# First block: gate2's second half on ScalarE and GpSimd, and the second routing pieces of both token tiles side by side

## The chip, the core and the metric

The kernel runs on one core of a Trainium2 chip. The metric is the device time of one execution in microseconds (us); the median of three runs is quoted, and one further execution was profiled. Engines are named as in the profile: PE (TensorE matmul), DVE (VectorE), ACT (ScalarE), POOL (GpSimd) and SP, whose queue issues nearly all loads from HBM.

## The reference, cut to what matters

Two blocks run one after the other over 256 tokens of width 1024. The first is attention and a pooling mixer, gated, followed by a mixture of 32 experts; the second is another mixer and an MLP, twice. The change touches the end of the first block's mixer, where the residual is formed, the router reads it, and the gate of the expert output is computed from the condition vector `c`.

```
mod = silu(c) @ w_ada + b_ada                       # six rows of 1024
shift1, scale1, gate1, shift2, scale2, gate2 = split(mod, 6)
...
x  = x + gate1 * (mixed @ w_out)
h2 = rms_norm(x, norm2_g) * (1 + scale2) + shift2
z_group, z_expert = h2 @ w_router_group + b, h2 @ w_router_expert + b
...                                                 # best group, best two of its eight experts
x  = x + gate2 * sum over the chosen experts e of weight_e * ((silu(h2 @ w_g[e]) * (h2 @ w_u[e])) @ w_d[e])
```

`gate2` is the vector c_act (1024) times a 1024 x 1024 slice of `w_ada`, computed in two halves of 512 columns. The routing needs, for each token, the sum of squares of the new x and 36 dot products of x with the router's weights.

## The kernel before, in words

Tokens stand on partitions in two tiles of 128 (t = 0, 1), and x has two column pieces of 512 (n = 0, 1). A float32 weight is split into a high part (`wh`, a cast on ACT, L206) and a low part (`wl`, a subtraction on DVE, L207), and each product is three matmuls: high with high (L230), low activation with high (L231), high activation with low weight (L232).

**Loads.** All weights pass through a ring of slots in SBUF, loaded by SP's queue in program order (`load_into`, L176). A slot is loaded again when its last reader is done, and SP waits in order: a load whose slot is still read holds every load behind it. While the first block's mixer (`phase_a`) still computes, the expert weights of `phase_b` are already being loaded, first the gate, up, gate and down matrices of the first experts (1 MB each), then 2 MB loads. The second 2 MB load of "up" goes into the slot that has held x until then (`self.xring`, added after `choose`), so it waits for the last reader of x.

**The end of phase_a.** The output projection `w_out` runs over two column pieces (c0 = 0, 512) and two halves of k. After each piece `evac_o` makes x: a product with gate1 (L723, reads PSUM) and a sum (L724). Between the matmuls the callback `both` advances two things: an order of steps (`start_route`, which makes the router's bias row zb from s2b, L867 and L870, then `route_piece` for n = 0 of both token tiles) and the generator `gate_sums` for gate2. For each half n of gate2 that generator lets GpSimd write the bias on a diagonal (L854, tile `gate2s`), then `ada_sum` loads two 1 MB parts of w_ada (four k rows each) and DVE adds eight scaled rows (L843, 128x512, one instruction per k row), and a matmul with ones (L858, `gb`) sums over partitions.

For c0 = 512 the last half of k is done token tile by token tile: t = 0 and its `evac_o`, t = 1 and its `evac_o`. Then `route_piece(t, 1, p)` runs for t = 0 and then t = 1: the sum of squares on ACT (`junk`, L270), four transposes on PE (`xt`, L884), a copy out of PSUM (`xa`, L886: on DVE for t = 0, on ACT for t = 1), four products with the router's weights (`lg`, L889), the reciprocal root on GpSimd (L278, L281), and the logits `z` on DVE (L892).

**The start of phase_b.** Four matmuls put x into the accumulators (`acc`, L986). `choose` picks experts on DVE (L906 to L927, result A); `slots` ranks tokens (L934 to L943). Then four ACT instructions make the high part of the normed x (L996), and four DVE instructions the low part (`low`, L1001): one behind A, three behind the comparison `sel` (L1041). After these the gather matmuls (`gx`, L1015) and the expert products run.

**Order of work.** Program order is only a priority: a scheduler places each instruction on its engine's queue where its own estimate of times has the engine free and the inputs ready. So on an engine a later step can stand before an earlier one. In the profile L854 for n = 1 stands on GpSimd directly behind that for n = 0, although eight DVE sums lie between them in program order, and L858 for n = 0 stands between the zb matmuls. `issue_after(ins)` puts an instruction behind `ins` on its engine. Once queued, each engine works strictly in order.

Of the kernel before, what the change touches and what calls it, by code (L numbers as in the profile page):

```python
# [11 lines left out]
F32 = mybir.dt.float32  # L12
# [4 lines left out]
AF = mybir.ActivationFunctionType  # L17
ALU = mybir.AluOpType
# [3 lines left out]
S = 256  # L22
D = 1024
# [92 lines left out]
class Kernel:  # L116
# [149 lines left out]
    def sumsq(self, x, ss, junk=None, scale=1.0):  # L266

        if junk is None:
            junk = self.sp.tile([128, D], F32R, name="junk", tag="wl")
        self.nc.scalar.activation(junk[:, 0:x.shape[1]], x, AF.Square, scale=scale, accum_out=ss)  # L270

    def rsqrt(self, ss, parts, n=D):

# [13 lines left out]
    def bank(self, shape=(128, 512), name="b"):  # L287
        return self.psum.tile(list(shape), F32, name=name, tag="b")
# [93 lines left out]
    def phase_a(self, rs):  # L382
        tc, nc, a = self.tc, self.nc, self.a
        with ExitStack() as st:
# [8 lines left out]
            p = s2.enter_context(tc.tile_pool(name="pa2", bufs=1, reuse_waits="tile"))  # L393
# [3 lines left out]
            bank = self.bank  # L397
# [11 lines left out]
            for t in range(2):  # L409
                ss = self.new_ss(1)  # L410
# [307 lines left out]
            p = st.enter_context(tc.tile_pool(name="pa3", bufs=1, reuse_waits="tile"))  # L718

            def evac_o(t, c0, ps):  # L720
                tmp = p.tile([128, 512], F32, name="otmp", tag="s", bufs=3)
                xx = self.x[:, t, c0:c0 + 512]
                nc.vector.tensor_tensor(tmp, ps, gate1[:, c0:c0 + 512], op=ALU.mult)  # L723
                nc.vector.tensor_tensor(xx, tmp, xx, op=ALU.add)  # L724


            self.gb = []
            sums = self.gate_sums(p.tile([128, D], F32, name="gate2s"), 10, lambda y, pb: self.gb.append(pb))

            def both():  # L730
                step()
# [3 lines left out]
            for c0 in (0, 512):  # L735
                ps = [bank() for _ in range(2)]
# [12 lines left out]
            for t in range(2):  # L749
                for k, hi, lo, off in parts:  # L750
                    self.tok_step1(ps[t], mT, 4 + k, t, hi[:, off:off + 512], lo[:, off:off + 512], False, k == 3)
                evac_o(t, 512, ps[t])
            for t in range(2):
                self.route_piece(t, 1, p)
    def load_rotary(self, p, tmp):
        a = self.a
        self.ind = self.cp.tile([128, 2], F32, name="ind")
        self.load_small(self.ind, a["k_rot"][:, 32:34])
        pos = p.tile([128, 2], I32, name="pos")
        self.load_small(pos, a["positions_2"].rearrange("o (t p) -> p (o t)", p=128))  # L760
        self.load_small(tmp[:, 194:226], a["k_rot"][:, 0:32])
        return pos, tmp
# [68 lines left out]
        self.row_cols(mod, pt, nb)  # L831
        self.nc.vector.tensor_reduce(dst, pt.rearrange("p b (i s r) -> p i b s r", s=2, r=32)[:, :, :, :, 0], axis=AX.X, op=ALU.add)

    def ada_sum(self, chunk, y, first):

        for i in range(2):
            v = self.ada_load(i, chunk)
            for kk in range(4):
                ck = self.cs[:, 4 * i + kk:4 * i + kk + 1]
                if first and i + kk == 0:  # L840
                    self.nc.vector.tensor_scalar(y, v[:, kk], ck, None, op0=ALU.mult)
                else:
                    self.nc.vector.scalar_tensor_tensor(y, v[:, kk], ck, y, op0=ALU.mult, op1=ALU.add)  # L843
                if kk % 2:
                    yield

    def gate_sums(self, gate, chunk, put):

        nc = self.nc
        c = self.vcol["b_ada", 16] + 4 * chunk - 16  # L850
        for n in range(2):
            y = gate[:, n * 512:(n + 1) * 512]

            nc.gpsimd.tensor_tensor(y.rearrange("p (b f) -> p b f", f=128), self.ident.unsqueeze(1).to_broadcast([128, 4, 128]),  # L854
                                    self.cols[:, c + 4 * n:c + 4 * n + 4].unsqueeze(2).to_broadcast([128, 4, 128]), op=ALU.mult)
            yield from self.ada_sum(chunk + n, y, False)
            pb = self.bank(name="gb")
            nc.tensor.matmul(pb, self.ones, y, start=True, stop=True)  # L858
            put(y, pb)
# [17 lines left out]
    def route_piece(self, t, n, p):  # L877

        nc, bank = self.nc, self.bank
        x = self.x[:, t, n * 512:n * 512 + 512]  # L880
        self.sumsq(x, self.ss1[t][:, n:n + 1])
        ps = bank((128, 4, 128), "xt")
        for b in range(4):
            nc.tensor.transpose(ps[:, b], self.strided(x, 4)[:, b], self.ident)  # L884
        xa = p.tile([128, 4, 128], F32, name="xa", tag="s", bufs=3)
        (nc.scalar.copy if t else nc.vector.tensor_copy)(xa, ps)  # L886
        for b in range(4):
            k = 4 * n + b
            nc.tensor.matmul(self.lg[t], xa[:, b], self.wr[:, k], start=k == 0, stop=k == 7)  # L889
        if n == 1:  # L890
            self.r1[t] = self.rsqrt(self.ss1[t], 2)
            nc.vector.scalar_tensor_tensor(self.z[:, t], self.lg[t], self.r1[t], self.br, op0=ALU.mult, op1=ALU.add)  # L892

    def choose(self, p):

# [77 lines left out]
    def phase_b(self, rs):  # L973
        tc, nc, a, misc = self.tc, self.nc, self.a, self.misc
        with ExitStack() as st:
            self.add_ring(rs, 1, side="right")
            p = st.enter_context(tc.tile_pool(name="pb", bufs=1, reuse_waits="tile"))
# [9 lines left out]
                                     skip_group_check=True)  # L987
            self.choose(p)
            Rm, cnt = self.slots(p)
            lows = []  # L990
            for n in range(2):
                for t in range(2):
                    xx = self.strided(self.x[:, t], 8)[:, 4 * n:4 * n + 4]
                    hi, lo = (self.hT.t[i][n][:, t] for i in range(2))
                    hi, lo = (v.rearrange("p (b c) -> p b c", b=4) if len(v.shape) == 2 else v for v in (hi, lo))
                    nc.scalar.activation(hi, xx, AF.Copy, scale=self.r1[t])  # L996
                    lows.append((lo, xx, self.r1[t], hi.bitcast(F32)))

            def low(after):
                with tc.issue_after(after):  # L1000
                    nc.vector.scalar_tensor_tensor(*lows.pop(0), op0=ALU.mult, op1=ALU.subtract)  # L1001

            low(self.after_A)

            self.add_slots(st, [self.xring])

# [29 lines left out]
            def choose_slots(pr):  # L1036

                b = pr // 2
                sel = [pw.tile([128, 4, 64], F32R, name="sel", tag=f"sel{t}") for t in range(2)]
                for t in range(2):  # L1040
                    cmp = nc.vector.tensor_tensor(sel[t], Rm[:, t, 4 * b:4 * b + 4].unsqueeze(2).to_broadcast([128, 4, 64]),  # L1041
                                                  misc[:, 0:64].unsqueeze(1).to_broadcast([128, 4, 64]), op=ALU.is_equal).ins
                while lows:
                    low(cmp)
                quad["sf"] = [s.rearrange("p e c -> p (e c)") for s in sel]
                quad["xT"] = pw.tile([128, 8, 256], F32, name="xT", tag="xT")

# [18 lines left out]
            def gate(pr):  # L1066

                pg = None
                if pr % 2 == 0:
                    choose_slots(pr)  # L1070
                for k in range(0, 10, 2):
                    if pr % 2 == 0 and k < 8:
                        gather(k)
                    if k:
                        if pg is None:
                            pg = self.bank((128, 512), "pg")
                        for kk in (k - 2, k - 1):
                            product(pg, weights["g", pr], pr, kk)
                    yield pg
# [822 lines left out]
```

## Time and profile before

| | us |
|---|---|
| Median of three runs | 1307.24 |
| Lowest and highest run | 1305.76, 1309.66 |
| The profiled execution | 1306.97 |
| Its span, first to last instruction | 1305.2 |
| Busy in the span: PE, DVE, ACT, POOL | 1253.0, 680.5, 510.7, 200.7 |
| HBM read in the span | 357.00 MB, 274 GB/s on average |

The times on the views count from the span's start. A timeline line gives the start, the duration, the engine, the line of code, the operation and "output<-inputs" with shapes; "x8" merges eight of a kind, and brackets at the end give idle time before it and what ended it. A windows line gives for a stretch the busy time of each engine with the number of instructions, then PE's granted clock as a share of full speed, the share of the DMA engines that were busy, and GB/s. A few records are missing from a trace of this kind, so counts on timelines can be one short.

### The profile page before, as it was taken

Reading aid. Unit: us, or ns where it says so; the run is one execution under the profiler, and the core shown is the slowest. Engines: PE = TensorE matmul, PEld = TensorE weight load, DVE = VectorE, ACT = ScalarE, POOL = GpSimd, SP = SyncE. Lnnn points to the kernel's source line nnn. Section 1 sums busy time; section 2 is a strip of 40 time slices with the busy share of each in tenths; the row PEclk is TensorE's granted clock in tenths of the full one; section 3 lists DMA queues with packets and bytes.
Section 4 is the critical chain, followed back from the end, with each engine's and each line's share of the span. In section 5 each row is a group of like instructions: output and inputs, shape, how many; then the busy total and the mean of one; then the engine's idle time right before and its main releaser. Section 6 shows DMA issues by size and latency. Waiting matters only on the chain. (4 is left out here: it accounts for less than half of the span.)

```text
span 1305.2 us, 19758 instructions
## 1 busy us (share of the span) xinstructions
PE 1253.0 (96%) x7985; PEld 875.2 (67%) x7985; DVE 680.5 (52%) x1164; ACT 510.7 (39%) x919; POOL 200.7 (15%) x270
## 2 busy tenths in 40 slices
PE   6999988999999999899999999999999999999997
PEld 3889976344443443333357678998988767989896
DVE  3698797122122221212157965655557994765654
ACT  2456433111110111101056465555556555655544
POOL 0011030000000000000024541211113461211211
PEclk9999998999999999999999999999999999999999
DMA  9998797999999999999975342655554423555550
GB/s 326 372 340 276 266 381 266 409 416 429 426 429 427 426 427 427 426 428 421 419 305 187 114 130 90 223 181 186 193 193 158 161 82 126 188 177 193 193 162 33
DMA packets 102597, 359.37 MB, mean 275 GB/s; under 512 B 8772, under 2 KB 17856, under 8 KB 87656
## 3 DMA queue, kind: packets, MB, share of 16 engines
q1 hardware_dynamic: 101832, 357.00, 72.1%
q8 instruction: 63, 1.03, 0.3%
q0 software_dynamic: 480, 1.07, 0.2%
q14 instruction: 30, 0.25, 0.1%
q10 hardware_dynamic: 192, 0.02, 0.0%
HBM read 357.00 MB, written 1.06 MB: 274 GB/s over the span
## 5 line engine op out<-in xcount | busy, mean ns | idle before, releaser
L207 DVE TENSOR_TENSOR wl<-w,wh 128x1024 fp32r<-128x1024 f32 x128 | 156.5, 1227 | 100.9 <-ACT wh L206 100.9
L206 ACT CAST wh<-w 128x1024 fp32r<-128x1024 f32 x128 | 134.1, 1050 | 144.4 <-PE up L241 65.8
L202 ACT ACTIVATE wh<-w,vcols 128x512 fp32r<-128x512 f32 x176 | 121.2, 718 | 78.9 <-PE dn L231 34.7
L203 DVE SCALAR_TENSOR_TENSOR wl<-w,vcols,wh 128x512 fp32r<-128x512 f32 x176 | 131.1, 778 | 36.5 <-ACT wh L202 34.4
L241 PE MATMUL up<-hT,wh 128*128 128x256 f32 x512 | 142.4, 278 | 0.0
L242 PE MATMUL up<-hT,wl 128*128 128x256 f32 x512 | 142.4, 279 | 0.0
L240 PE MATMUL up<-hT,wh 128*128 128x256 f32 x512 | 142.4, 278 | 0.0
L1015 PE MATMUL pu<-w,xT 128*64 128x512 f32 x512 | 121.5, 608 | 5.4 <-DMA w<-in_w_expert_up_dram 5.4
L1015 PE MATMUL pg<-w,xT 128*64 128x512 f32 x512 | 119.5, 604 | 0.0
L1101 ACT CAST yh<-y 128x512 fp32r<-128x512 f32 x32 | 19.8, 618 | 253.6 <-DVE y L1100 187.9
L1015 PE MATMUL py<-w,actT 128*64 128x512 f32 x480 | 108.0, 593 | 1.4 <-DMA w<-in_w_expert_down_dram 1.4
L231 PE MATMUL dn<-wh,actl 128*128 128x512 f32 x256 | 101.3, 396 | 0.0
L230 PE MATMUL dn<-wh,acth 128*128 128x512 f32 x256 | 101.2, 395 | 0.0
L232 PE MATMUL dn<-wl,acth 128*128 128x512 f32 x256 | 101.2, 396 | 0.0
L241 PEld LDWEIGHTS up<-hT,wh 128*128 128x128 f32 x512 | 96.9, 189 | 0.6
L240 PEld LDWEIGHTS up<-hT,wh 128*128 128x128 f32 x512 | 96.2, 188 | 0.6
L242 PEld LDWEIGHTS up<-hT,wl 128*128 128x128 f32 x512 | 96.0, 188 | 0.5 <-DVE wl L203 0.5
L1803 POOL TENSOR_TENSOR relu<-relu 128x256 f32<-128x256 f32 x64 | 53.6, 838 | 265.9 <-ACT relu L1802 265.9
L230 PE MATMUL b<-wh,hT 128*128 128x512 f32 x224 | 92.0, 412 | 2.4 <-ACT wh L202 1.9
L232 PE MATMUL b<-wl,hT 128*128 128x512 f32 x224 | 89.4, 403 | 2.3 <-DVE wl L207 1.5
L1100 DVE SCALAR_TENSOR_TENSOR y<-py,ws,gate 128x512 f32<-128x512 f32 x30 | 22.5, 751 | 128.7 <-PE py L1015 127.2
L1015 PEld LDWEIGHTS pu<-w,xT 128*64 128x64 f32 x512 | 38.0, 139 | 76.9 <-issue 67.1
(411 smaller groups left out, 2273.3 us busy)
## 6 DMA issues: line engine op xcount, KB each, us to landing
w<-in_w_expert_up_dram SPq DMA_DIRECT2D x26, 2048.0 KB, 25.7
w<-in_w_expert_down_dram SPq DMA_DIRECT2D x26, 2048.0 KB, 27.2
w<-in_w_expert_gate_dram SPq DMA_DIRECT2D x24, 2048.0 KB, 25.4
w<-in_w_in_dram SPq DMA_DIRECT2D x40, 1024.0 KB, 6.5
w<-in_w_up_dram SPq DMA_DIRECT2D x32, 1024.0 KB, 5.4
w<-in_w_down_dram SPq DMA_DIRECT2D x32, 1024.0 KB, 5.0
w<-in_w_ada_dram SPq DMA_DIRECT2D x24, 1024.0 KB, 9.8
w<-in_w_expert_gate_dram SPq DMA_DIRECT2D x16, 1024.0 KB, 10.3
```

The source lines that it names most:

```text
L202: self.nc.scalar.activation(hi[:, c], v[:, c], AF.Copy, scale=g[:, i:i + 1])
L203: self.nc.vector.scalar_tensor_tensor(lo[:, c], v[:, c], g[:, i:i + 1], hi[:, c].bitcast(F32), op0=ALU.mult, op1=ALU.subtract)
L206: self.last_hi = self.nc.scalar.copy(hi, v).ins
L207: self.last_lo = self.nc.vector.tensor_tensor(lo, v, hi, op=ALU.subtract).ins
L230: nc.tensor.matmul(ps, hT.tok(0, k, t), wh, start=first, stop=False)
L231: nc.tensor.matmul(ps, hT.tok(1, k, t), wh, start=False, stop=False)
L232: nc.tensor.matmul(ps, hT.tok(0, k, t), wl, start=False, stop=last)
L240: nc.tensor.matmul(o, hi[:, c], hT.mov(0, k), start=first and m % 2 == 0, stop=False, skip_group_check=True)
L241: nc.tensor.matmul(o, hi[:, c], hT.mov(1, k), start=False, stop=False, skip_group_check=True)
L242: nc.tensor.matmul(o, lo[:, c], hT.mov(0, k), start=False, stop=last and m % 2 == 1, skip_group_check=True)
L1015: queue["last"] = f(*args, **kw).ins
L1803: nc.gpsimd.tensor_tensor(r, r, r, op=ALU.mult)
```

## The change

Two parts. First, for gate2's second half (n = 1) the eight DVE sums of 128x512 are gone. For each k row and each half of 256 columns, ACT writes the scaled row into a temporary (six buffers, shared with other temporaries of that pool), and GpSimd adds it to `gate2s`: 16 ACT instructions and 16 GpSimd instructions of 128x256. Second, `route_end` replaces the two `route_piece(t, 1, p)`: sums of squares, transposes and copies of both token tiles come first, both copies on DVE; then products, reciprocal root and logits of each; then the four ACT instructions of the normed x (L996 before), which are told to stand behind the sum of squares of t = 1. In `phase_b` only the `low` instructions remain. The same instructions otherwise; nothing else of the kernel differs.

```diff
-            sums = self.gate_sums(p.tile([128, D], F32, name="gate2s"), 10, lambda y, pb: self.gb.append(pb))
+            sums = self.gate_sums(p.tile([128, D], F32, name="gate2s"), 10, lambda y, pb: self.gb.append(pb),
+                                  lambda: ft([128, S], F32, "gt"))
...
-            for t in range(2):
-                self.route_piece(t, 1, p)
+            self.route_end(p)
...
                 ck = self.cs[:, 4 * i + kk:4 * i + kk + 1]
-                if first and i + kk == 0:
+                if scaled:
+                    for c in (slice(0, S), slice(S, 2 * S)):
+                        tmp = scaled()
+                        self.nc.scalar.activation(tmp, v[:, kk, c], AF.Copy, scale=ck)
+                        self.nc.gpsimd.tensor_tensor(y[:, c], y[:, c], tmp, op=ALU.add)
+                elif first and i + kk == 0:
...
-            yield from self.ada_sum(chunk + n, y, False)
+            yield from self.ada_sum(chunk + n, y, False, scaled if n else None)
...
+    def route_end(self, p):
+
+        nc, bank = self.nc, self.bank
+        self.lows, xas = [], []
+        for t in range(2):
+            x = self.x[:, t, 512:1024]
+            sq = self.sumsq(x, self.ss1[t][:, 1:2])
+            ps = bank((128, 4, 128), "xt")
+            for b in range(4):
+                nc.tensor.transpose(ps[:, b], self.strided(x, 4)[:, b], self.ident)
+            xa = p.tile([128, 4, 128], F32, name="xa", tag="s", bufs=3)
+            nc.vector.tensor_copy(xa, ps)
+            xas.append(xa)
+        for t in range(2):
+            for b in range(4):
+                nc.tensor.matmul(self.lg[t], xas[t][:, b], self.wr[:, 4 + b], start=False, stop=b == 3)
             self.r1[t] = self.rsqrt(self.ss1[t], 2)
             nc.vector.scalar_tensor_tensor(self.z[:, t], self.lg[t], self.r1[t], self.br, op0=ALU.mult, op1=ALU.add)
+        for n in range(2):
+            for t in range(2):
+                self.normed(t, n, sq)
+
+    def normed(self, t, n, after):
+
+        xx = self.strided(self.x[:, t], 8)[:, 4 * n:4 * n + 4]
+        hi, lo = (self.hT.t[i][n][:, t] for i in range(2))
+        hi, lo = (v.rearrange("p (b c) -> p b c", b=4) if len(v.shape) == 2 else v for v in (hi, lo))
+        with self.tc.issue_after(after):
+            self.nc.scalar.activation(hi, xx, AF.Copy, scale=self.r1[t])
+        self.lows.append((lo, xx, self.r1[t], hi.bitcast(F32)))
...
-            low(self.after_A)
+            self.low(self.after_A)
```

## Rows read from the trace of the kernel before

**Rows 1.** Windows: columns PE, PEld, DVE, ACT, POOL, clock, DMA share, GB/s.

```profile
183.00:195.00 12.00, 9.08 (x38) 6.71 (x37) 11.95 (x19) 4.48 (x8) 3.20 (x5) 1.00 1.01 409
233.00:253.00 20.00, 20.00 (x98) 7.17 (x98) 2.24 (x5) 2.81 (x4) 0.00 (x0) 1.00 1.01 408
```

**Rows 2.** Waits: total us, times, longest; SP 150 to 260, PE 235 to 700.

```profile
SPq L176 <- DVE gate2s L843: 21.7, 3, 8.9
SPq L176 <- DVE hT L1001: 8.4, 1, 8.4
...
PE pu L1015 <- DMA w<-in_w_expert_up_dram: 5.4, 2, 2.7
```

**Rows 3.** Timeline of the DMA queue SP: start, us, what (three answers).

```profile
202.38 0.33 SPq L176 DMA_DIRECT2D w<-in_w_expert_down_dram  x1
210.62 0.80 SPq L176 DMA_DIRECT2D w<-in_w_expert_down_dram  x2
226.00 0.33 SPq L176 DMA_DIRECT2D w<-in_w_expert_up_dram  x1
```

**Rows 4.** The tile gate2s: the instructions that add to it, ns min/median/max.

```profile
L843 DVE SCALAR_TENSOR_TENSOR gate2s<-w,cs,gate2s x16: 740/746/753, 183.2 to 209.8; 128x512 f32<-128x512 f32 x16
```

**Rows 5.** Groups by form, first 235 us, GpSimd and ScalarE (mean ns).

```profile
L707 POOL TENSOR_TENSOR t<-t,t 128x256 f32<-128x256 f32 x8 | 7.5, 958 | 47.0 <-DVE t L706 47.0
L533 ACT ACTIVATE zs<-b,vcols 128x256 f32<-128x256 f32 x16 | 6.6, 478 | 2.4 <-PE b L242 2.3
```

**Rows 6.** Timeline of GpSimd: start, us, what.

```profile
161.10 1.87 POOL L707 TENSOR_TENSOR t<-t,t 128x256 f32<-128x256 f32 x2 [34.98 <-DVE t L706]
183.62 2.45 POOL L670 DMA_DIRECT2D sae<-sa  x4 [0.66 <-DVE sa L666]
826.01 1.06 POOL L1803 TENSOR_TENSOR relu<-relu 128x256 f32<-128x256 f32 x1 [0.91 <-ACT relu L1802]
```

**Rows 7.** Timeline of VectorE beside the GpSimd work of the group above.

```profile
161.59 0.42 DVE L706 TENSOR_TENSOR t<-b,zs 128x256 f32<-128x256 f32 x1
826.52 0.83 DVE L310 TENSOR_TENSOR actl<-relu,acth 128x256 fp32r<-128x256 f32 x1
828.41 0.41 DVE L310 TENSOR_TENSOR actl<-relu,acth 128x256 fp32r<-128x256 f32 x1
```

**Rows 8.** Timeline of VectorE, 165 to 235.

```profile
186.84 0.74 DVE L843 SCALAR_TENSOR_TENSOR gate2s<-w,cs,gate2s 128x512 f32<-128x512 f32 x1
194.49 0.76 DVE L867 COPY s2b<-sa 128x512 f32<-128x512 f32 x2
209.85 0.75 DVE L843 SCALAR_TENSOR_TENSOR gate2s<-w,cs,gate2s 128x512 f32<-128x512 f32 x1
210.51 0.69 DVE L723 TENSOR_TENSOR otmp<-b,xres 128x512 f32<-128x512 f32 x1
212.41 0.69 DVE L886 COPY xa<-xt 128x512 f32<-128x512 f32 x1 [0.47 <-PE xt L884]
217.06 0.26 DVE L892 SCALAR_TENSOR_TENSOR z<-lg,rs,br 128x36 f32<-128x36 f32 x1 [2.21 <-PE lg L889]
```

**Rows 9.** Timeline of ScalarE, 165 to 235.

```profile
212.41 2.33 ACT L996 ACTIVATE hT<-xres,rs 128x512 fp32r<-128x512 f32 x2 [1.72 <-POOL rs L281]
215.25 0.56 ACT L886 COPY xa<-xt 128x512 f32<-128x512 f32 x1
```

**Rows 10.** Timeline of TensorE, 193 to 222: the zb step, then the tail.

```profile
194.97 1.08 PE L870 MATMUL zb<-xres,s2b 128*128 128x36 f32 x8 [1.37 <-DVE s2b L867]
209.41 0.39 PE L232 MATMUL b<-wl,hT 128*128 128x512 f32 x1
210.74 1.10 PE L858 MATMUL gb<-gate2s,ones 128*128 128x512 f32 x2 [0.94 <-DVE gate2s L843]
211.68 1.13 PE L884 MATMUL xt<-ident,xres 128*128 128x128 f32 x8
215.87 1.08 PE L889 MATMUL lg<-xres,xa 128*128 128x36 f32 x8 [1.38 <-ACT xa L886]
```

More of the change, by code (lines that the diff above doesn't have):

```diff
@@ L269, in sumsq @@
             junk = self.sp.tile([128, D], F32R, name="junk", tag="wl")
-        self.nc.scalar.activation(junk[:, 0:x.shape[1]], x, AF.Square, scale=scale, accum_out=ss)
+        return self.nc.scalar.activation(junk[:, 0:x.shape[1]], x, AF.Square, scale=scale, accum_out=ss).ins
     def rsqrt(self, ss, parts, n=D):
@@ L832, in halves_cols, with ada_sum @@
         self.nc.vector.tensor_reduce(dst, pt.rearrange("p b (i s r) -> p i b s r", s=2, r=32)[:, :, :, :, 0], axis=AX.X, op=ALU.add)
-    def ada_sum(self, chunk, y, first):
+    def ada_sum(self, chunk, y, first, scaled=None):
         for i in range(2):
@@ L845, in ada_sum, with gate_sums @@
                     yield
-    def gate_sums(self, gate, chunk, put):
+    def gate_sums(self, gate, chunk, put, scaled=None):
         nc = self.nc
@@ L889, in route_piece, with low @@
             nc.tensor.matmul(self.lg[t], xa[:, b], self.wr[:, k], start=k == 0, stop=k == 7)
-        if n == 1:
+    def route_end(self, p):
[13 more added lines that the diff above has]
+                nc.tensor.matmul(self.lg[t], xas[t][:, b], self.wr[:, 4 + b], start=False, stop=b == 3)
             self.r1[t] = self.rsqrt(self.ss1[t], 2)
             nc.vector.scalar_tensor_tensor(self.z[:, t], self.lg[t], self.r1[t], self.br, op0=ALU.mult, op1=ALU.add)
+        for n in range(2):
[8 more added lines that the diff above has]
+        self.lows.append((lo, xx, self.r1[t], hi.bitcast(F32)))
+    def low(self, after):
+        with self.tc.issue_after(after):
+            self.nc.vector.scalar_tensor_tensor(*self.lows.pop(0), op0=ALU.mult, op1=ALU.subtract)
     def choose(self, p):
@@ L989, in phase_b @@
             Rm, cnt = self.slots(p)
[L990 to L1001, printed above, removed]
-            low(self.after_A)
+            self.low(self.after_A)
             self.add_slots(st, [self.xring])
@@ L1042, in choose_slots @@
                                                   misc[:, 0:64].unsqueeze(1).to_broadcast([128, 4, 64]), op=ALU.is_equal).ins
-                while lows:
-                    low(cmp)
+                while self.lows:
+                    self.low(cmp)
                 quad["sf"] = [s.rearrange("p e c -> p (e c)") for s in sel]
```

## The prediction

> **What bounds the kernel now.** I started from the page. The slices of the span show the DMA engines full from about 235 us to 650 us, while the expert weights stream in, and PE waiting only now and then in that stretch. The windows give the same in numbers: from 233 to 253 us the DMA share is 1.01 [rows 1]. The waits of PE between 235 and 700 us are short, and the longest in total is for a transfer of expert weights, 5.4 us [rows 2]. So the transfers set the pace of the long middle part, and its end moves with the moment at which the queue last ran dry. The waits of the DMA queue then show what holds the loads before that: its largest item is the tile gate2s, 21.7 us in three waits, because slots that hold w_ada come free only when DVE has added the last row. Behind that stands one wait of 8.4 us for the low part of the normed x [rows 2]. The queue's timeline shows which one is the last. The issue at 210.62 waits for gate2s, and the one at 226.00, into the slot that held x, waits for the last instruction L1001 [rows 3]. It is the last for which the queue runs dry. What the change is worth is therefore read from that one path: last matmul of w_out, x of token tile 1, its routing piece, logits, choice of experts, low part, load at 226.00.
>
> The path in numbers: the last matmul of w_out for t = 1 starts at 209.41 and takes 0.39, so it ends at 209.80 [rows 10]. The logits z of t = 1 start at 217.06 [rows 8]. From there to the issue at 226.00 [rows 3] it is 8.9 us, of instructions that the change leaves as they are. Between 209.80 and 217.06 lie 7.3 us, and a reader can see three things there that need not be on the path. DVE does a sum for gate2s at 209.85, ahead of L723 of t = 1 at 210.51 [rows 8]. PE has the matmul gb at 210.74, which waits for that sum and stands ahead of the transposes xt at 211.68 [rows 10]. And ACT does two instructions L996 for token tile 0 (2.33 us from 212.41) before it comes to the sum of squares and, at 215.25, to the copy xa of tile 1 [rows 9].
>
> **The tail, from 209.80 to z.** With the sums off DVE and the copies side by side, the steps for t = 1 are: handover 0.06 (xa ends at 215.81, lg starts at 215.87 [rows 9, 10]), L723 and L724 of one form at 0.69 each, 1.4 together [rows 8], from xt to xa 0.73 (211.68 to 212.41 [rows 8, 10]), xa on DVE 0.69 [rows 8], handover 0.06, and from lg to z 1.19 (215.87 to 217.06 [rows 8, 10]). That is 4.1 us instead of 7.3, a gain of 3.2. The reciprocal root runs beside xa and lg. Moving xa from ACT to DVE is counted (0.69 for 0.56). The copy of tile 0 may fall between L723 and L724 of tile 1 (0.7 lost), and a matmul of 1.1 such as gb or acc may still stand before xt. So the gain lies between 1.4 and 3.2, and I take 3.2, since PE and DVE have little else to do there once the sums are gone. The four L996 now stand behind the second sum of squares. They take 4 x 1.17 = 4.7 us on ACT and are done before the low parts need them: the first waits for A, some 3 us behind z.
>
> **The sums on GpSimd and ScalarE.** Eight of the 16 sums L843 (0.746 us each [rows 4]) leave DVE. They are those of n = 1, and all stand behind the copies s2b at 194.49 [rows 8], so before that DVE has the same work as now. ACT gets 16 pieces of 128x256; the nearest form takes 478 ns [rows 5], 7.6 us in all. ACT is busy 4.48 of 12 us from 183 to 195 [rows 1], and I cost the pieces at nothing. If that cover were gone, because a piece waits for one of six temporaries that an add must first release, the casts of w_out weights behind it on ACT would be late by one add, about 1 us. GpSimd gets 16 adds. The nearest form, L707, has a mean of 958 ns [rows 5], so the chain is 15.3 us long. w_ada has been loaded long before, and its bias instruction L854 is done by 183, so I expect the adds to be queued at once, behind the four descriptors of L670, which end at 186.07 [rows 6]. None of the loads, which are earlier by several us at 202.38 and 210.62, shortens the path, because the queue waits for x's slot after them anyway.
>
> What the adds cost is on DVE. The rows show that a two-input DVE instruction on SBUF and a GpSimd add don't stream together: beside the add at 826.01 (1.06 us) [rows 6] the DVE subtraction at 826.52 takes 0.83, and the same form without one takes 0.41 [rows 7]. So each add that meets such an instruction holds DVE for 0.42. The product at 161.59, which reads PSUM and one SBUF tile, takes its usual 0.42 in the middle of an add [rows 6, 7]. From 183 to 195 us DVE is busy 11.95 of 12 us [rows 1], and PE waits for it: the zb matmuls at 194.97 have stood idle for 1.37 us until s2b came [rows 10]. Between 186.84 and s2b DVE starts 11 instructions (first and last neighbour in [rows 8]), of which two are products from PSUM. From 186.07 to 194.49, in 8.4 us, 8 or 9 adds fit, and 9 of 11 partners can be held, so about 7 holds of 0.42: s2b comes 2.9 us later. PE works without a gap from zb to 209.80, so the end of w_out comes 2.9 us later too. The bounds: no hold at all, if the adds fall into gaps or after s2b; all 16 in front of work that PE waits for, 6.7 us. I take 2.9, since DVE shows no gaps there.
>
> One rule of the Trainium skill goes further than these rows. "GPSIMD Engine Reference", section "Specifications", says that GpSimd shares its SBUF interfaces with VectorE, and that contention is with DVE instructions that have two SBUF inputs or run in a 2-port mode. The first half agrees with the rows above (0.83 against 0.41), and no row here shows the second half. If the two s2b copies are of that second kind, two more holds make 0.8 us, and the sum below would be 1307.5.
>
> **Sum.** Minus 3.2 for the tail, plus 2.9 for DVE: minus 0.3 us. The profiled execution took 1306.97, so 1306.7. It stands 0.27 below the median of 1307.24, which makes no difference here. A measurement of this kernel tells about 0.3% (3.9 us) from no change, that is, under 1303.1 or over 1310.9.
>
> **Rivals.** (1) The holds don't reach the path: adds are queued late, or PE has slack before zb. Then the tail's 3.2 stays, and one L843 less before the next weight split gives up to 0.75: 1303.0 to 1303.8. A short idle PE in the tail may add a little more, so 1302.5 at best. For it: PE is idle 1.37 us before zb; against it: DVE is full from 183 to 195 [rows 1, 10].
>
> (2) Slower: the new matmul gb waits for GpSimd in the middle of w_out. The scheduler's estimate may know nothing of the holds and put gb on PE's queue soon behind zb. The chain ends at 186.07 + 16 x 0.96 = 201.4, or at 203.0 if each add takes the 1.06 of the held one [rows 5, 6]. PE, which would be there at about 199, stands up to 4.0 us and then does gb (1.1), all of it before the end of w_out: 1.1 to 5.1 us on top of the sum, 1307.8 to 1311.8. It decides where gb is queued over 3 us before the last add ends; then it is 1310.5 or more. For it: now gb stands in PE's order where its sums are expected to end [rows 10]. Against it: half of w_out's matmuls could as well be put in front.
>
> (3) The earlier loads themselves count: the queue issues nothing between 202.38 and 210.62 [rows 3], and 1 MB takes about 2.6 us at 408 GB/s [rows 1], so 5.6 us of dry time could be saved: 1301.4. Against it: x's slot at 226.00 comes after it.
>
> **How the numbers follow.** The forecast, a wash, has 0.47 and its own range is 1304.5 to 1309.5 (tail 1.4 to 3.2, holds between 1 and 4 us). Rival 1 has 0.30, a bit over half of it below 1303.1 when the runs' spread is counted; rival 2 has 0.18, about half above 1310.9; rival 3 has 0.05, all below. That makes faster 0.22, slower 0.12, the same 0.66. The range runs from 1302.3 to 1311.2: it leaves out rival 3 and the upper end of rival 2.
>
> **What would show it.** Right, if L207 and L724 between 186 and 195 grow by about 0.4 each beside GpSimd adds of 1 us; s2b starts near 197; w_out ends near 212.7; z of t = 1 follows 4.1 us after it; the load into x's slot is issued near 225.7. Wrong, if DVE keeps its durations there (rival 1), if PE has a wait for gate2s on GpSimd before the end of w_out (rival 2), or if x's slot is no longer the last load that the queue waits for with nothing in flight (rival 3).

## The result, and the profile after

The changed kernel takes 1320.08 us, the median of four runs (1318.17 to 1320.83), against 1307.24. The ratio of the two kernels is given as 1.0091 with a 95% interval of 1.0077 to 1.0106, a little less than the quotient of the two medians (1.0098). So it is slower by about 12 us. The experiments below are compared by such ratios, each against runs of the kernel before that were made beside it, because that kernel's own median lies between 1307.2 and 1309.4 from one set of runs to the next. The prediction said 1306.7 with a range that ended at 1311.2, so it was wrong, and on the side to which it gave a chance of 0.12. The profiled execution took 1318.17, which is 11.2 us more than that of before.

The path that the prediction had picked is the right one, and it can be followed moment by moment in both traces (starts and ends in us; the last column says how much the delay grew or shrank since the row above):

| | before | after | step of the difference |
|---|---|---|---|
| second copy s2b ends | 195.25 | 204.91 | +9.7 |
| last matmul of w_out ends | 209.80 | 223.46 | +4.0 |
| z of t = 1 starts | 217.06 | 228.43 | -2.3 |
| load into x's slot issued | 226.00 | 237.31 | -0.1 |
| last product of the experts added up | 673.6 | 684.1 | -0.8 |

So the whole loss is there before the expert stage, and the expert stage carries it to the end. The first step is on DVE. Its timeline of the changed kernel, columns as in [rows 8]:

```profile
183.11 0.68 DVE L666 SCALAR_TENSOR_TENSOR sa<-sa,xres 128x8 f32<-128x8 f32 x1
183.72 1.28 DVE L849 SCALAR_TENSOR_TENSOR gate2s<-w,cs,gate2s 128x512 f32<-128x512 f32 x1
184.93 1.75 DVE L207 TENSOR_TENSOR wl<-w,wh 128x1024 fp32r<-128x1024 f32 x1
186.59 1.22 DVE L849 SCALAR_TENSOR_TENSOR gate2s<-w,cs,gate2s 128x512 f32<-128x512 f32 x1
187.73 2.11 DVE L207 TENSOR_TENSOR wl<-w,wh 128x1024 fp32r<-128x1024 f32 x1
...
193.73 0.68 DVE L723 TENSOR_TENSOR otmp<-b,xres 128x512 f32<-128x512 f32 x1
194.33 6.12 DVE L849 SCALAR_TENSOR_TENSOR gate2s<-w,cs,gate2s 128x512 f32<-128x512 f32 x1
200.37 0.68 DVE L724 TENSOR_TENSOR xres<-otmp,xres 128x512 f32<-128x512 f32 x1
200.97 0.74 DVE L849 SCALAR_TENSOR_TENSOR gate2s<-w,cs,gate2s 128x512 f32<-128x512 f32 x1
...
204.16 0.75 DVE L873 COPY s2b<-sa 128x512 f32<-128x512 f32 x2
```

Two of the same instructions in the kernel before:

```profile
183.17 0.15 DVE L666 SCALAR_TENSOR_TENSOR sa<-sa,xres 128x8 f32<-128x8 f32 x1
187.50 1.22 DVE L207 TENSOR_TENSOR wl<-w,wh 128x1024 fp32r<-128x1024 f32 x1
```

A sum L849 is the L843 of before: 0.74 there [rows 8], 1.2 to 1.3 here four times. The weight split L207 took 1.21 to 1.22 before and takes 1.75, 2.11 and 1.75 here. L723, which reads PSUM and one SBUF tile, keeps its 0.68. And one sum takes 6.12 us. What GpSimd did meanwhile, in two answers of its timeline:

```profile
182.99 2.60 POOL L845 TENSOR_TENSOR gate2s<-gate2s,gt 128x256 f32<-128x256 f32 x3
185.54 2.45 POOL L670 DMA_DIRECT2D sae<-sa  x4
188.01 11.89 POOL L845 TENSOR_TENSOR gate2s<-gate2s,gt 128x256 f32<-128x256 f32 x13
201.90 0.18 POOL L278 TENSOR_SCALAR ms<-ss 128x1 f32<-128x1 f32 x1 [2.01 <-ACT junk L270]
```
```profile
L845 POOL TENSOR_TENSOR gate2s<-gate2s,gt x16: 712/733/1733, 183.0 to 199.2; 128x256 f32<-128x256 f32 x16
L849 DVE SCALAR_TENSOR_TENSOR gate2s<-w,cs,gate2s x8: 735/1215/6120, 183.7 to 203.5; 128x512 f32<-128x512 f32 x8
```

The second fence is the view of the tile gate2s, which answers to [rows 4] (ns, min/median/max). The adds begin at 182.99, before the descriptors, and all 16 are over by 199.90. Beside a held DVE instruction an add takes up to 1.73, and 0.71 to 0.74 in the row of adds that ran while the long sum stood. The sum of 194.33 ended at 200.45, half a microsecond after the last add: the last eight adds ran back to back while it stood. From 200.97 on, with GpSimd idle, DVE has its old durations again.

The account adds up: the small step L666 of 183.11 took 0.68 for 0.15 (0.5), four sums 2.0 in all, three L207 another 2.0, the long sum 5.4 (6.12 less 0.74). That is 9.9 us for the 9.7 that s2b is late.

The second step is on PE. The windows of the changed kernel, columns as in [rows 1], the first of them answering to its first row:

```profile
183.00:195.00 12.00, 8.84 (x31) 6.73 (x31) 12.00 (x11) 6.44 (x12) 11.98 (x13) 0.86 0.90 351
195.00:205.00 10.00, 2.06 (x10) 1.41 (x8) 10.00 (x10) 4.35 (x8) 5.08 (x9) 0.83 0.51 200
205.00:215.00 10.00, 10.00 (x33) 7.89 (x33) 4.56 (x6) 0.00 (x0) 0.00 (x0) 0.50 0.95 362
```
```profile
PE zb L876 <- DVE s2b L873: 7.9, 1, 7.9
PE b L230 <- ACT wh L206: 2.2, 1, 2.2
```

From 183 to 195 DVE is as full as before (12.00 for 11.95) but starts 11 instructions instead of 19, and GpSimd is busy 11.98 instead of 3.20. Then PE waits 7.9 us for s2b, against 1.37 before [rows 10], and after that wait its granted clock is 0.50, which is 1.2 GHz, through the whole window from 205 to 215. So the stretch from s2b to the end of w_out takes 18.55 us instead of 14.55, although PE stands idle nowhere in it. Part of this is also the matmul gb of the second half (219.09, 1.10 us with its two passes), which stood behind w_out before [rows 10]; e7 below divides the two.

The tail did shrink, from 7.26 us to 4.97:

```profile
223.50 0.69 DVE L723 TENSOR_TENSOR otmp<-b,xres 128x512 f32<-128x512 f32 x1 [1.39 <-PE b L232]
224.10 0.68 DVE L908 COPY xa<-xt 128x512 f32<-128x512 f32 x1
224.70 0.68 DVE L724 TENSOR_TENSOR xres<-otmp,xres 128x512 f32<-128x512 f32 x1
```

The copy of tile 0 stands between L723 and L724 of tile 1, which the prediction had named as a loss of 0.7.

### The profile page after: what moved, and what is told of

Same layout as the page of the kernel before. It is cut to its first block, busy times and chain, and to the rows that moved or that the text cites. A ratio compares the mean times of both kernels' runs of the same rounds, so it can differ in the third digit from the quotient of the medians.

```text
span 1316.4 us, 19796 instructions
## 1 busy us (share of the span) xinstructions
PE 1253.7 (95%) x7985; PEld 880.1 (67%) x7985; DVE 685.9 (52%) x1157; ACT 517.3 (39%) x934; POOL 217.7 (17%) x286
## 5 line engine op out<-in xcount | busy, mean ns | idle before, releaser
L207 DVE TENSOR_TENSOR wl<-w,wh 128x1024 fp32r<-128x1024 f32 x128 | 158.1, 1240 | 100.3 <-ACT wh L206 100.3
L206 ACT CAST wh<-w 128x1024 fp32r<-128x1024 f32 x128 | 133.9, 1049 | 137.2 <-PE up L241 65.9
L1040 PE MATMUL pu<-w,xT 128*64 128x512 f32 x512 | 118.4, 596 | 5.5 <-DMA w<-in_w_expert_up_dram 5.5
L230 PE MATMUL b<-wh,hT 128*128 128x512 f32 x224 | 93.1, 417 | 4.5 <-ACT wh L206 2.2
L231 PE MATMUL b<-wh,hT 128*128 128x512 f32 x224 | 90.3, 403 | 0.0
```

What stands on the lines that cost most here:

```text
L206: self.last_hi = self.nc.scalar.copy(hi, v).ins
L207: self.last_lo = self.nc.vector.tensor_tensor(lo, v, hi, op=ALU.subtract).ins
L230: nc.tensor.matmul(ps, hT.tok(0, k, t), wh, start=first, stop=False)
L231: nc.tensor.matmul(ps, hT.tok(1, k, t), wh, start=False, stop=False)
L1040: queue["last"] = f(*args, **kw).ins
```

## The experiments

**The theory** after the result: the GpSimd adds hold DVE's two-input instructions ahead of s2b, PE stands idle for s2b, and its clock falls. **Rivals:** ScalarE's pieces delay the casts of w_out's weights; the new order of the tail costs; merely having the sums in a new place (ahead of PE's matmul gb) costs; the clock, and not the holds, is the bulk.

**e1: the sums alone.** The sums as in the change, the routing as before (the lines are against the changed kernel).

```diff
...
-            self.route_end(p)
+            for t in range(2):
+                self.route_piece(t, 1, p)
...
```

> The kernel before with the sums part of the change alone (ScalarE scales, GpSimd adds), routing as before. Theory A (GpSimd's adds hold VectorE, the copies s2b come 9.7 us late, TensorE then runs 7 us longer at the low clock; the routing part gains 2.3 us): slower than the changed kernel by about 2.3 us, so 13 to 14 us over before, with one VectorE sum held for about 6 us behind GpSimd adds without gaps. Theory B (the two parts harm each other, say by the order that the scheduler makes of both): within 4 us of before.

Measured: 1320.09 us, ratio 1.0089 (1.0059 to 1.0119). s2b ended at 204.73, and the same sum was held for as long, on its line of DVE's timeline:

```profile
194.15 6.12 DVE L849 SCALAR_TENSOR_TENSOR gate2s<-w,cs,gate2s 128x512 f32<-128x512 f32 x1
```

The sums alone make the whole loss. The 2.3 us more than in the change that theory A had expected, for want of the new routing, did not come: z of t = 1 follows the end of w_out after 5.48 us here, against 4.97 in the change.

**e2 and e10: the routing alone**, the second time for a narrower interval.

```diff
-            yield from self.ada_sum(chunk + n, y, False, scaled if n else None)
+            yield from self.ada_sum(chunk + n, y, False, None)
```

> The changed kernel with gate2's second half summed on VectorE as before; only the routing part is left. Theory A: 2 to 3 us faster than before (1304 to 1305), w_out ends near 209.8 us, z of the second token tile starts 4.2 to 5 us later. Theory B: within 1 us of before or slower, because the order of ScalarE's normed x or of the accumulator matmuls gives the gain back before the load into x's slot.

> The routing part alone once more, with more rounds, to settle its sign. From the first runs of it: 0.05% to 0.25% faster than before, 1304 to 1307; if the side by side order is worth nothing, 0.1% around before.

Measured: 1306.37 us, ratio 0.9988 (0.9971 to 1.0006), and 1308.38, ratio 0.9990 (0.9977 to 1.0004). Each is about a thousandth faster, and neither interval leaves out no change. In both profiles z of t = 1 comes 5.7 us after the end of w_out (7.26 before), so 1.6 us of the tail come from the new order, as far as two profiles tell.

**e3: the 16 adds on DVE. e4: no adds at all** (ScalarE still makes the 16 pieces).

```diff
-                        self.nc.gpsimd.tensor_tensor(y[:, c], y[:, c], tmp, op=ALU.add)
+                        self.nc.vector.tensor_tensor(y[:, c], y[:, c], tmp, op=ALU.add)
...
-                        self.nc.gpsimd.tensor_tensor(y[:, c], y[:, c], tmp, op=ALU.add)
```

> The changed kernel, but the 16 adds stand on VectorE instead of GpSimd; ScalarE still scales. Theory A (GpSimd's hold on VectorE is the loss): back to before or 2 to 3 us faster, 1303 to 1307, no VectorE instruction near s2b over 1.3 us long. Theory B (the pieces on ScalarE and its casts that stand behind them are the loss): most of the 13 us stays, 1315 or more.

> The changed kernel without the 16 GpSimd adds (the second half of gate2 lacks its sum); ScalarE still writes the scaled pieces. Theory A: the whole loss goes and VectorE is relieved of its eight sums behind s2b: 1302 to 1305. Theory B (ScalarE's pieces or the new order): 1315 or more.

Measured: 1310.14 us, ratio 1.0006 (0.9987 to 1.0024), and 1308.08, ratio 0.9996 (0.9977 to 1.0016). Both are like the kernel before; the gain that theory A expected of them (1303 to 1307 and 1302 to 1305) did not come. So nearly the whole 0.9% comes with the adds on GpSimd. What the pieces themselves cost is small and can be read in e4: s2b ends at 196.76, 1.5 us later than before, since the casts L206 stand behind pieces on ACT and PE, after its wait for one of them, has a granted clock of 0.86 from 183 to 195 (1.00 before [rows 1]). The waits of PE in e4, 180 to 215:

```profile
PE zb L875 <- DVE s2b L872: 1.4, 1, 1.4
PE b L230 <- ACT wh L206: 0.9, 1, 0.9
```

In e3 DVE does the adds behind s2b. Its stretch starts 2.0 us late in this profile (the first sum at 185.16 for 183.20 in e4), and from there s2b comes at the same distance as in e4: 13.5 us, from 185.16 to 198.70, and 13.6, from 183.20 to 196.76.

**e5: one temporary instead of six**, so that an add and the next piece take turns and GpSimd stands still between adds.

```diff
-            sums = self.gate_sums(p.tile([128, D], F32, name="gate2s"), 10, lambda y, pb: self.gb.append(pb),
-                                  lambda: ft([128, S], F32, "gt"))
+            one = []
+
+            def gt():
+                if not one:
+                    one.append(ft([128, S], F32, "gt"))
+                return one[0]
+
+            sums = self.gate_sums(p.tile([128, D], F32, name="gate2s"), 10, lambda y, pb: self.gb.append(pb), gt)
```

> The changed kernel with a single temporary for the scaled pieces instead of six, so that GpSimd has to wait for ScalarE between two adds, and the scheduler puts the last six adds behind the sums of squares. Theory A1 (adds that are queued without a gap keep VectorE out; with a gap it gets in): no VectorE instruction near s2b over 2.2 us, s2b done by 197 to 201 instead of 204.9, total 1309 to 1315. Theory A2 (each add costs VectorE its own length wherever it falls): the sum of the holds stays, s2b at 203 or later, 1317 or more.

Measured: 1309.93 us, ratio 1.0009 (0.9994 to 1.0023). The loss is gone. GpSimd's and DVE's timelines:

```profile
196.97 1.13 POOL L851 TENSOR_TENSOR gate2s<-gate2s,gt 128x256 f32<-128x256 f32 x1 [0.62 <-ACT gt L850]
```
```profile
196.06 0.83 DVE L855 SCALAR_TENSOR_TENSOR gate2s<-w,cs,gate2s 128x512 f32<-128x512 f32 x1
196.81 0.68 DVE L724 TENSOR_TENSOR xres<-otmp,xres 128x512 f32<-128x512 f32 x1
197.42 1.23 DVE L855 SCALAR_TENSOR_TENSOR gate2s<-w,cs,gate2s 128x512 f32<-128x512 f32 x1
...
200.53 1.29 DVE L879 COPY s2b<-sa 128x512 f32<-128x512 f32 x2
```

With a gap of 0.62 us between adds no instruction of DVE is held by more than one add (1.23 for 0.74), and the last adds come behind s2b. s2b still ends at 201.82, 6.6 us late, but PE's order is another here: from 183 to zb it has 49 of w_out's matmuls to do instead of 36, waits only 0.6 us for s2b (and 4.6 for a cast), keeps a clock of 1.00 from 195 to 215, and ends w_out at 214.01. So a late s2b costs the time that PE stands idle for it, not its own delay, and this run does not tell what the gaps alone are worth: two things changed, the holds and PE's order. The two s2b copies take 1.29 instead of the 0.76 of [rows 8].

**e6: the pieces behind the sums of squares**, so that the adds come after s2b.

```diff
-                self.tok_part(ps, mT, wo, 0, c0, True, False, both)
+                self.tok_part(ps, mT, wo, 0, c0, True, False, step if c0 else both)
...
-                        self.nc.scalar.activation(tmp, v[:, kk, c], AF.Copy, scale=ck)
+                        with self.tc.issue_after(self.last_sq):
+                            self.nc.scalar.activation(tmp, v[:, kk, c], AF.Copy, scale=ck)
...
-        self.sumsq(x, self.ss1[t][:, n:n + 1])
+        self.last_sq = self.sumsq(x, self.ss1[t][:, n:n + 1])
```

> The changed kernel with the pieces told to stand behind the sum of squares of the first routing pieces on ScalarE, so that all adds come after s2b. Theory A: s2b is back at 194 to 196 and no long idle time of TensorE comes before zb; the adds then run from about 195 to 208 and hold the last weight splits and copies, and the matmul gb, which stands inside w_out on TensorE's queue, waits for them: w_out ends at 210 to 214, 1305 to 1312. Theory B (the adds cost the same wherever they stand): 1317 or more.

Measured: 1312.32 us, ratio 1.0023 (1.0009 to 1.0037). s2b ends at 194.60, the same as before, since this execution is 0.66 us early as a whole at 180. The 16 adds then run from 195.86 to 209.68, and PE meets them:

```profile
209.74 1.12 PE L865 MATMUL gb<-gate2s,ones 128*128 128x512 f32 x2 [4.23 <-POOL gate2s L846]
```

This is the prediction's second rival, in the place that it gave and just above its price (up to 4.0 us): gb stands in the middle of w_out and waits for the chain on GpSimd. It needed the adds to be late; in the change they were too early for it.

**e7: PE kept busy.** Ten matmuls whose result nobody reads stand ahead of zb (the scheduler also moved four of w_out's matmuls behind zb).

```diff
+        wb = bank((128, 512), "warm")
+        for _ in range(10):
+            warm = nc.tensor.matmul(wb, self.ones, self.xbuf[:, 2048:2560], start=True, stop=True).ins
...
-                nc.tensor.matmul(ps, s2b[:, b], self.wr[:, k], start=k == 0, stop=k == 7)
+                with self.tc.issue_after(warm):
+                    nc.tensor.matmul(ps, s2b[:, b], self.wr[:, k], start=k == 0, stop=k == 7)
```

> The changed kernel with ten matmuls of 128x512 whose result nobody reads, ahead of zb on TensorE, so that TensorE is busy while it waits for s2b. Theory A (a third of the loss is the low clock after the idle time): s2b stays near 204.9, the granted clock is 1.0 after it, w_out ends near 219 to 220 instead of 223.5, 1313 to 1316. Rival: the time from zb to the end of w_out is long for another reason (the matmul gb, the casts): 1318 or more.

Measured: 1316.28 us, ratio 1.0053 (1.0036 to 1.0069), below the interval of the change. The window that showed 0.50 above:

```profile
205.00:215.00 10.00, 10.00 (x56) 7.84 (x55) 5.39 (x9) 0.51 (x3) 0.00 (x0) 1.00 0.84 319
```

The clock is 1.00 (2.4 GHz) here, and from s2b to the end of w_out PE takes 15.3 us instead of 18.6, although s2b is as late as in the change (205.83, in an execution that is 0.9 us late as a whole at 180). That is 3.2 us of the profile; the two ratios differ by 0.38%, some 5 us.

The 3.2 is not the whole price of the clock, since e7 has the four matmuls more (0.9 us) in that stretch and starts zb 0.4 us behind s2b. The better comparison is e4, where PE has the same matmuls between s2b and the end of w_out as in the change, both gb among them:

```profile
195.00:205.00 10.00, 8.63 (x52) 7.28 (x52) 6.42 (x10) 1.77 (x6) 3.33 (x1) 1.00 1.01 410
205.00:215.00 10.00, 9.09 (x51) 6.90 (x50) 4.21 (x7) 3.34 (x7) 1.84 (x5) 1.00 0.59 247
```

At a clock of 1.00 it takes 13.7 us there, from 196.76 to 210.43, so the low clock costs the change 4.9 of its 18.6. The kernel before lost some of this too: 14.55 against 13.1 in e2, which has its matmuls there in the same place and a clock of 1.00. Of the 4.0 us by which the stretch grew, 3.4 are therefore the clock and 0.6 the matmul gb. The rest of the loss is the delay of s2b itself, 9.7 us, less the 2.3 us that the tail gave back.

**e8: GpSimd copies in place of the adds**, with one input instead of two (gate2's second half is then the last piece).

```diff
-                        self.nc.gpsimd.tensor_tensor(y[:, c], y[:, c], tmp, op=ALU.add)
+                        self.nc.gpsimd.tensor_copy(y[:, c], tmp)
```

> The changed kernel with each GpSimd add replaced by a GpSimd copy of the piece, one input instead of two (the second half of gate2 is then the last piece, not the sum). Theory A3 (any stream of GpSimd through SBUF keeps a two-input VectorE instruction out): holds of VectorE remain, 1313 or more. Theory A4 (only the two inputs of the add do): as without adds, 1306 to 1310, no VectorE instruction near s2b over 1.3 us.

Measured: 1312.75 us, ratio 1.0028 (1.0013 to 1.0043). GpSimd and DVE:

```profile
189.44 6.08 POOL L845 COPY gate2s<-gt 128x256 f32<-128x256 f32 x12
```
```profile
193.58 2.48 DVE L849 SCALAR_TENSOR_TENSOR gate2s<-w,cs,gate2s 128x512 f32<-128x512 f32 x1
```

One-input instructions of GpSimd hold DVE too, each for less (the sums beside them take 0.88 to 0.94, for 0.74). The sum behind L723 is again the one that is kept waiting, here by the copies that were left, and s2b ends at 200.53, 5.3 us later than before, of which 1.4 are the execution as a whole (at 180).

**e9: a constant in place of the pointer scalar** in DVE's sums for the first half of gate2, since only sums with one had been held for long.

```diff
-                    self.nc.vector.scalar_tensor_tensor(y, v[:, kk], ck, y, op0=ALU.mult, op1=ALU.add)
+                    self.nc.vector.scalar_tensor_tensor(y, v[:, kk], 0.5 if chunk == 10 else ck, y, op0=ALU.mult, op1=ALU.add)
```

> The changed kernel with a constant 0.5 in place of the per-partition scalar from SBUF in VectorE's eight sums of gate2's first half (that half is then wrong); orders on all engines as in the changed kernel. Theory S1 (the pointer scalar is what lets the adds overtake the sum behind the product from PSUM): the sum near 194.4 us is held for one add, 1.3 us or less, s2b near 200, 1310 to 1314. Theory S2 (what a VectorE instruction reads beside its two tiles does not matter; adds without a gap keep it out once they are ahead): a hold of about 6 us again, 1317 to 1321.

Measured: 1316.07 us, ratio 1.0056 (1.0040 to 1.0072), with three runs, which is below the interval of the change and between the times of the two theories. DVE at the place of the long hold:

```profile
195.80 0.68 DVE L849 SCALAR_TENSOR_TENSOR gate2s<-w,gate2s 128x512 f32<-128x512 f32 x1
196.40 1.23 DVE L724 TENSOR_TENSOR xres<-otmp,xres 128x512 f32<-128x512 f32 x1
197.54 1.23 DVE L849 SCALAR_TENSOR_TENSOR gate2s<-w,gate2s 128x512 f32<-128x512 f32 x1
...
202.17 1.81 DVE L873 COPY s2b<-sa 128x512 f32<-128x512 f32 x2
```

The long hold is gone, and DVE and GpSimd take turns to the end; but the adds now last until 206.23, hold L724 and the s2b copies as well, and s2b ends at 203.98. This execution was some 2 us late as a whole at 183 us, so set against the change it is about 202. As far as one profile tells, taking turns costs most of s2b's delay by itself, and the long hold only some 3 us more. Whether it is the pointer scalar that lets a DVE sum be passed over by several adds stays open.

**e11 and e12: the s2b copies on ScalarE**, on top of e2 and on the kernel before alone.

```diff
-            nc.vector.tensor_copy(s2b, self.s2[:, 4 * n:4 * n + 4].unsqueeze(2).to_broadcast([128, 4, 128]))
+            nc.scalar.copy(s2b, self.s2[:, 4 * n:4 * n + 4].unsqueeze(2).to_broadcast([128, 4, 128]))
```

> The routing part alone, and the two copies s2b on ScalarE instead of VectorE, so that zb no longer waits for VectorE's queue. If s2b on VectorE's queue is where the loss entered (theory A), TensorE's idle 1.4 us before zb and the low clock behind it go: the load into x's slot 1 to 3 us earlier than with the routing part alone, 1302 to 1306, 0.1% to 0.4% faster than before. Rival: the next weight split on VectorE is late instead, and nothing changes: within 0.1% of the routing part alone.

> The kernel before with the two copies s2b on ScalarE and nothing else. Theory A: 1 to 2 us faster than before, and slower than the same with the routing part by 1 to 3 us. Rival: the same as before.

Measured: 1306.53 us, ratio 0.9983 (0.9972 to 0.9994), and 1305.22, ratio 0.9969 (0.9957 to 0.9981). ScalarE and PE in e12:

```profile
191.15 1.14 ACT L867 COPY s2b<-sa 128x512 f32<-128x512 f32 x2
```
```profile
192.98 0.97 PE L870 MATMUL zb<-xres,s2b 128*128 128x36 f32 x8
```

The copies end at 192.28 instead of 195.25, zb starts without a wait, where it stood 1.37 us before [rows 10], and the load into x's slot is issued at 223.1 instead of 226.00. The clock from 195 to 205 is 1.00 here, for 0.83 before. e12 is 0.3% faster than the kernel before and has the lowest ratio of this study. It was expected to be 1 to 3 us slower than e11, and it is not: the intervals of the two overlap, and although e11 issues that load 1.5 us earlier (221.62), its profiled time is 1.3 us longer. So the new routing shows no gain on top.

## Why the prediction was wrong

**Right: the path.** It said that the time hangs on the load into x's slot, by way of s2b, PE from zb to the end of w_out, and the tail. The load moved by 11.3 us and the profiled time by 11.2. In all fourteen profiles the last product of the experts ends 447 to 451 us after this load is issued, and what follows takes 633 to 636 us, so up to some 3 us between two profiles can arise behind it: e2 issued the load 3.0 us earlier than before and was 0.3 us shorter. The third rival is not tested by the change, although the queue's wait for gate2s fell from 21.7 us [rows 2] to 13.4: the queue then waited longer for other slots (16.3 us for lg, 5.5 before, and 9.9 for s2b, 4.4 before). e3 is nearer to it: from 202 to 210 us the DMA share was 0.98 there, for 0.52 before, and the time was that of the kernel before.

**Right in mechanism, short in size: the tail.** Forecast -3.2 with bounds of 1.4 and 3.2, measured -2.3, with the copy of tile 0 where the bound had put it. e1 has 5.48 us with the routing as before, so most of the gain comes from DVE being free of sums there; the new order adds 0.5 on top, and 1.6 when it is alone (e2).

**Wrong: the holds on DVE, 2.9 us with a bound of 6.7.** This is the step that failed. It measured 9.7. Three things in it were wrong. First, the count: I took the adds that fit into the 8.4 us that remained until s2b before, seven holds. But each hold makes that time longer, so that more adds fit into it, and in the end all 16 came ahead of s2b. That is a loop, not a stretch of fixed length: where two engines take turns, the number of holds is bounded by the work of the other engine alone. Second, the start: I put the adds behind the four descriptors of L670; three stood ahead of them, from 182.99. Third, the size, "each add that meets such an instruction holds DVE for 0.42": it was 0.5 where they took turns (once 0.9), and a sum was passed over by eight adds in a row, 5.4 us. The upper bound was short for that: 16 x 0.42 took the cheapest row for every add; 9.7 over 16 adds is 0.60 each.

**Wrong: "so the end of w_out comes 2.9 us later too".** I let the end of w_out move with s2b, one for one. The idle time before zb grew from 1.4 to 7.9 us, and the clock went to 0.50 afterwards, which the prediction had nowhere. With e4 and e2 beside it this is 3.4 us more than the kernel before lost to its clock; e7 got 3.2 of the profile back. A view of before could have warned, its windows behind the idle 1.37 us:

```profile
195.00:205.00 10.00, 10.00 (x55) 8.41 (x56) 8.88 (x13) 0.59 (x1) 0.30 (x1) 0.83 0.98 390
```

The clock is 0.83 of full speed on the mean here, so a part of the window ran at 1.2 GHz. It need not: e2 and e10 are the same kernel with the same wait of 1.4 us at this place, and e2 has 1.00 in this window and takes 13.1 us from s2b to the end of w_out, e10 has 0.66 and takes 16.1.

**Wrong by a little: the pieces on ScalarE at nothing.** The casts behind them were late: 1.5 us at s2b in e4. The prediction had priced this at about 1 us if the cover was gone. The median of e4 shows no loss.

**The second rival** saw a slower kernel for another reason, and its mechanism exists: e6 shows it with 4.2 us. In the change itself gb of the second half waited for nothing, since the adds had ended 19 us earlier. One sum of the prediction is a little off, without effect: a tail of 1.4 to 3.2 and holds of 1 to 4 us give 1304.8 to 1309.6, not 1304.5 to 1309.5.

The prediction quoted the Trainium skill, "GPSIMD Engine Reference", section "Specifications", for two kinds of DVE instruction that contend with GpSimd. The first kind, with two SBUF inputs, the traces bear out again and again (0.74 against 1.22). For the second, the s2b copies may speak: they have one SBUF input, and two took 1.29 and 1.81 us beside adds (e5, e9), 0.75 without; but no view names the mode in which a copy runs. The Trainium skill, "SBUF — State Buffer", section "SBUF: two separate sides", says that whichever instruction starts first has the shared pair of ports for its whole length and the other one blocks. The turns agree with that (a hold of 0.5 us beside adds of 0.71). The hold of 5.4 us goes further than one instruction's length, and there the measurement decides. As a bound, a hold of a whole add for each of 16 would have been 11.4 us at the 0.71 measured here, an estimate by that page of the Trainium skill; it would have held the 9.7 us of s2b, but not the time, which needs the clock as well.

What stays open: why DVE and GpSimd take turns up to 193.7 and not behind that, why the sum at 186.59 took 1.22 beside the descriptors L670, when L207 took its usual 1.21 beside them before, and why a wait of 1.4 us leaves the clock high in one execution and low in another.

## What to carry to other kernels

Before work is moved from a full DVE to GpSimd, count every GpSimd instruction that could run beside two-input DVE instructions as one hold of about its own length (0.60 for an add of 0.71 us here), all of them and not only those that fit into the old stretch; where that is more than the DVE time saved in front of the wait that matters, leave it. If GpSimd must have it, leave gaps between its instructions (with one temporary instead of six no DVE instruction was held by more than one add, and the loss was gone, though PE's order had changed too), or put them where DVE has nothing urgent and no matmul waits for the result (e6). And look first at what the busy engine does for the waiting one: here two copies of 0.4 us each, moved to an engine that had time, gave 0.3%, where the routing part alone gave 0.1%, not told from nothing, and the whole change lost 0.9%.

## What the runs showed that was not expected

A DVE instruction with two SBUF inputs can be passed over by a row of GpSimd instructions: 6.1 us behind eight adds in the change, e1 and e7, and 2.48 us behind five shorter copies in e8, always the first sum that follows L723 (that sum took 0.83 with gaps between the adds, e5, and 0.68 with a constant, e9). After an idle PE of 7.9 us the granted clock stayed at 0.50 through the next ten microseconds although PE was busy throughout; with PE kept busy it was 1.00. After an idle 1.4 us the same kernel had 1.00 in one execution and 0.66 in another (e2, e10), so part of the spread between runs of one kernel may be this clock; that is not shown.
